# The order of one attention stage: value and gate projections together, the second front of the delta rule next, then the rotations and the attention

## The chip, the cores and the metric

One core of one Trainium2 chip runs the whole program in one launch. The metric is device time in microseconds (us), the median of the runs of a kernel. The engines named below are TensorE (PE, with its weight loads as PEld), VectorE (DVE), ScalarE (ACT), GpSimd (POOL) and SyncE (SP), whose queue issues nearly all DMAs.

## The reference

Two hybrid layers on 256 tokens of width 1024 come first, then one layer of a second kind, in which the change lies. Cut to what matters:

```python
zx = split(modulate(rmsnorm(x, g), ...) @ w_in)     # queries, keys, values, delta-rule inputs, gates
q, k = rmsnorm per head of zx[0], zx[1]; q, k = apply_axial_rope(q), apply_axial_rope(k)
o_a  = diff_attention(q, concat(k_ctx, k), concat(v_ctx, v), lam)     # 8 heads, two softmax maps each
scan_in = rwkv_prepare(zx[3], ...)                  # decay, kk, a, k, v, r of 16 heads, two directions
o_b  = rwkv_post(wkv_scan(s_ctx, scan_in), ...)     # s = s*w - (s@kk) (kk*a)^T + v k^T;  y = s @ r
x = x + mod * (sigmoid(g_a) * (o_a @ w_a) + sigmoid(g_b) * (o_b @ w_b)) @ w_out
x = x + mod * peer_ffn(...)                         # product-key experts, 128 x 128
```

## The kernel before

The program is written in the order of `body`: two layers of the first kind, then `second`, then the experts. The work of `second` on the main tokens runs in this order. `w_proj` and `z_proj` project the inputs of the delta rule and park them in DRAM (`zx`). The delta rule is done in two halves of eight heads, each by a `wkv_front` and a `wkv_back`:

- `wkv_front` (L1176) computes decays and keys for 8 blocks of 32 tokens in both directions, the Gram products of the blocks (L1300), the inverse of the 32 x 32 triangles by 31 elimination steps on DVE (a multiplication and a subtraction each, "the elimination" below; its input goes through DRAM as `din`, its result as `dout`, and L1333 transposes the result back), and the products that need the inverse.
- `wkv_back` (L1360) walks the 8 blocks in order, since the state `S` is carried. A step is L1376 (state times inputs, PE), an addition on DVE, L1392 (PE), an evacuation on ACT, L1404 (PE), and the addition and scaling of `S` on DVE. At the end L1420 adds what lies inside the blocks, and a group norm, L1446 and L1447 give the output `od`.

The attention has `da_front` (L1068: project and sum squares), `da_tail` (L1082: scale, rotate, transpose by L1108, store to DRAM), `v_unit` (L1126: 48 matmuls of 256 columns for a quarter of the values, stored to DRAM) and `gate2` (L1534: 48 matmuls, a tanh and one operation for an eighth of the gates). `diff_attention` (L1455) goes over 8 heads and two halves of the tokens, 16 items in all. An item's front is two score matmuls (L1476), two maxima (L1477), two exponentials (L1482), and L1488, which combines the two maps; its back is four transposes (L1494), an evacuation, four matmuls (L1499) and a scaling. The fronts run one item ahead of the backs. After the last item come a norm (L1520 to L1524), transposes (L1531) and the split into `hh` and `hl` (L394, L395), which `merge2` multiplies with `w_branch_a` ("ba"), then with `w_branch_b` ("bb").

In `second`, `da_tail` is a generator that yields after each quarter of the heads; the kernel before runs one `v_unit` after each quarter of the queries, and two `gate2` after each quarter of the keys. `wkv_front` and `wkv_back` are issued at a high priority, so the scheduler that sets the instruction order of each engine pulls them ahead as far as their buffers allow. Two buffers matter here: the second front writes its own `WR` into the tiles `hh` and `hl`, which the projections of values and gates read until their end, and it takes the tag `w8`, of which 9 buffers exist, so that a part of it waits until the first back has read its own.

Of the kernel before, what the change touches and what calls it, by code (L numbers as in the profile page):

```python
# [19 lines left out]
T = 256  # L20
# [174 lines left out]
class Kern:  # L195
# [1370 lines left out]
    def second(self, pool, xd):  # L1566
        nc, P = self.nc, self.P2
        self.rows2 = self.t(pool, [128, 384], "rows2")
        nc.sync.dma_start(self.rows2, self.A["rows2"].partition_broadcast(128))
        self.wkv_consts(pool)  # L1570
        dram = lambda shape, name: self.t(self.dram, shape, name)
        kTd, qTd, vd = dram([128, 8, 512], "kTd"), dram([128, 8, T], "qTd"), self.vd
        zx = dram([128, 24, T], "zx")
        gd, od = [dram([128, 8, T], f"gd{i}") for i in range(2)], dram([128, 8, T], "od")
        S = self.t(pool, [128, 2, 2, 4, 64], "S")
        for hf in range(2):
            nc.sync.dma_start(S[:, hf], self.Sd[hf])
        norm = lambda: [self.t(self.work, [128, 8, T], n, F32R) for n in ("hh", "hl")]
        hh, hl = self.ctx_front

        def back(state, S, od=None):
            with self.stream("r"), self.tc.high_priority(offset=30000):
                self.wkv_back(state, S, od)

        def front(*args):
            with self.stream("w"), self.tc.high_priority(offset=30000):
                return self.wkv_front(pool, *args)

        self.n4, self.n8 = 8, 9
        a = self.w8(pool, [128, 2, 16, 64])  # L1590
        fc = self.da_front(pool, a, "bk", hh, hl)
        nc.sync.dma_start(xd, self.x)
        hh, hl = norm()
        self.mod_norm(self.halves(self.x), P["norm1_g"], 0, 0, hh, hl, hold=True)
        wax, self.sg = self.w_proj(pool, 1, hh, hl)
        self.z_proj(pool, 1, hh, hl, zx)
        for _ in self.da_tail(pool, fc, self.rows2[:, 64:128], False, kTd, 0):
            pass
        st = front(1, 0, zx, wax)
        a = self.t(self.xp, [128, 2, 16, 64], "x")  # L1600
        fq = self.da_front(pool, a, "bq", hh, hl)
        a = self.t(self.xp, [128, 2, 16, 64], "xn", bufs=1)
        fk = self.da_front(pool, a, "bk", hh, hl)
        for i, _ in enumerate(self.da_tail(pool, fq, self.rope_tables(pool, self.rows2[:, 0:64], "tab"), True, qTd, 0)):
            self.v_unit(pool, i, hh, hl, vd, 2)
        for i, _ in enumerate(self.da_tail(pool, fk, self.rope_tables(pool, self.rows2[:, 64:128], "tab"), True, kTd, T)):
            for u in (2 * i, 2 * i + 1):
                g = self.gate2(pool, u, hh, hl)
                nc.sync.dma_start(gd[u // 4][:, 2 * (u % 4):2 * (u % 4) + 2], g)
        back(st, S[:, 0], od)  # L1610
        st = front(1, 1, zx, wax, True)
        hh, hl = norm()
        self.diff_attention(pool, kTd, qTd, vd, hh, hl)
        back(st, S[:, 1], od)
        M = self.t(self.xp, [128, 8, T], "xn", bufs=1)
        self.merge2(pool, M, "ba", gd[0], hh, hl)
        hh, hl = norm()
        for m in range(0, 8, 2):
            o = self.t(pool, [128, 2, T], "d2", bufs=4)
            nc.sync.dma_start(o, od[:, m:m + 2])  # L1620
            nc.scalar.activation(hh[:, m:m + 2], o, AF.Copy)  # L1621
            self.sub(hl[:, m:m + 2], o, hh[:, m:m + 2].bitcast(F32))
        self.merge2(pool, M, "bb", gd[1], hh, hl)
        hh, hl = norm()
        for m in range(0, 8, 2):
            nc.scalar.activation(hh[:, m:m + 2], M[:, m:m + 2], AF.Copy)
            self.sub(hl[:, m:m + 2], M[:, m:m + 2], hh[:, m:m + 2].bitcast(F32))
        self.x = self.t(self.xp, [128, 2, D], "x")
        nc.sync.dma_start(self.x, xd)
        g2 = [self.t(pool, [128, 512], "d2", bufs=4) for n in range(2)]  # L1630
        self.mod_rows(2, 0, g2)
        with self.stream("w"):
            pw = [self.bank_pair()]
        with self.stream("r"):
            pw.append(self.bank_pair())
        for i in range(4):
            self.linB_acc(f"bo{i}", pw, hh[:, 2 * i:2 * i + 2], hl[:, 2 * i:2 * i + 2], i == 0, i == 3)
        for t in range(2):
            for n in range(2):
                c = slice(512 * n, 512 * n + 512)  # L1640
                tp = self.t(pool, [128, 512], "d2", bufs=4)
                self.mul(tp, pw[t][n], g2[n])
                self.add(self.x[:, t, c], self.x[:, t, c], tp)
# [309 lines left out]
```

## Time and profile before

| what | value |
|---|---|
| median of 3 runs | 2797.48 us (2794.47 to 2798.41) |
| the profiled execution's own time | 2798.71 us |
| its span, first to last instruction | 2796.9 us |
| busy PE, PEld, DVE, ACT | 94%, 82%, 71%, 51% of the span |
| mean granted clock of TensorE | 0.946 of full speed |

The page says that PE is busy almost throughout, and that the mean clock is near full. A stage has to be read by itself: the page's row of granted clock shows two to four slices of forty well below full, and those lie in `second`, roughly from 1600 to 1800 us, where DMA moves less than half of what it moves elsewhere. The page's slices are 70 us wide, so finer windows are needed for the argument.

### The profile page before, as it was taken

Reading aid. Unit: us, or ns where it says so; the run is one execution under the profiler, and the core shown is the slowest. Engines: PE = TensorE matmul, PEld = TensorE weight load, DVE = VectorE, ACT = ScalarE, POOL = GpSimd, SP = SyncE. Lnnn points to the kernel's source line nnn. Section 1 sums busy time; section 2 is a strip of 40 time slices with the busy share of each in tenths; the row PEclk is TensorE's granted clock in tenths of the full one; section 3 lists DMA queues with packets and bytes.
Section 4 is the critical chain, followed back from the end, with each engine's and each line's share of the span. In section 5 each row is a group of like instructions: output and inputs, shape, how many; then the busy total and the mean of one; then the engine's idle time right before and its main releaser. Section 6 shows DMA issues by size and latency. Waiting matters only on the chain.

```text
span 2796.9 us, 54976 instructions
## 1 busy us (share of the span) xinstructions
PE 2635.9 (94%) x21856; PEld 2293.4 (82%) x21856; DVE 1978.4 (71%) x4085; ACT 1423.3 (51%) x2392; POOL 14.2 (1%) x45
## 2 busy tenths in 40 slices
PE   7999899999999999987998979989989999999999
PEld 7986588886997768877888755779989998888887
DVE  5996668765897658766788776566987765666665
ACT  4554446543555446534664655444446554444444
POOL 0000000000000000000000000000000000000000
PEclk9999999999999999988999976699999999999999
DMA  5532866546543555535746522264664346666665
GB/s 189 175 124 88 263 225 199 168 152 219 167 147 126 162 199 170 173 107 166 237 134 200 166 68 59 67 200 163 190 185 137 122 149 208 215 208 219 207 216 183
DMA packets 212433, 472.00 MB, mean 169 GB/s; under 512 B 52816, under 2 KB 86480, under 8 KB 211152
## 3 DMA queue, kind: packets, MB, share of 16 engines
q1 hardware_dynamic: 212176, 468.48, 52.4%
q8 instruction: 172, 2.82, 0.4%
q14 instruction: 85, 0.70, 0.1%
HBM read 427.77 MB, written 40.63 MB: 167 GB/s over the span
## 4 chain that ended last, share of the span: by engine, by line
PE 79%; DVE 10%; DMA 6%; ACT 4%; issue 2%; SPq 0%; DVEq 0%; ACTq 0%
PE a L333 8%; PE a L335 8%; PE a L334 8%; PE b L353 4%; PE b L351 4%; PE b L352 4%; PE b L1767 3%; PE x L335 3%; PE x L333 3%; PE x L334 3%; PE a L352 3%; PE a L351 3%; PE a L353 3%; DVE wl L277 3%; DMA raw<-in_peer 2%
## 5 line engine op out<-in xcount | busy, mean ns | idle before, releaser
L312 ACT ACTIVATE wh<-raw 128x1024 fp32r<-128x1024 f32 (+1 forms) x701 | 638.2, 913 | 689.3 <-PE a L334 247.4
L277 DVE TENSOR_TENSOR wl<-raw,wh 128x1024 fp32r<-128x1024 f32 (+1 forms) x701 | 727.4, 1041 | 357.9 <-ACT wh L312 332.6
L333 PE MATMUL a<-hh,wh 128*128 128x256 f32 x1920 | 550.2, 287 | 8.8 <-ACT hh L1621 4.1
L335 PE MATMUL a<-hh,wl 128*128 128x256 f32 x1920 | 549.5, 286 | 4.5 <-DVE wl L277 4.2
L334 PE MATMUL a<-hl,wh 128*128 128x256 f32 x1920 | 547.2, 285 | 0.6 <-DVE hl L277 0.5
L333 PEld LDWEIGHTS a<-hh,wh 128*128 128x128 f32 x1920 | 365.5, 190 | 22.0 <-ACT wh L312 4.9
L335 PEld LDWEIGHTS a<-hh,wl 128*128 128x128 f32 x1920 | 365.2, 190 | 14.8 <-DVE wl L277 9.0
L334 PEld LDWEIGHTS a<-hl,wh 128*128 128x128 f32 x1920 | 364.9, 190 | 5.4 <-DVE hl L277 0.7
L333 PE MATMUL x<-hh,wh 128*128 128x256 f32 x720 | 205.8, 286 | 5.6 <-ACT wh L312 5.2
L335 PE MATMUL x<-hh,wl 128*128 128x256 f32 x720 | 206.6, 287 | 3.0 <-DVE wl L277 3.0
L334 PE MATMUL x<-hl,wh 128*128 128x256 f32 x720 | 204.9, 285 | 0.0
L352 PE MATMUL b<-wl,ah 128*128 128x512 f32 x512 | 201.0, 393 | 0.0
L351 PE MATMUL b<-wh,ah 128*128 128x512 f32 x512 | 191.2, 393 | 2.8 <-issue 2.8
L353 PE MATMUL b<-wh,al 128*128 128x512 f32 x512 | 191.8, 391 | 0.0
L333 PEld LDWEIGHTS x<-hh,wh 128*128 128x128 f32 x720 | 137.2, 191 | 9.0 <-ACT wh L312 6.7
L335 PEld LDWEIGHTS x<-hh,wl 128*128 128x128 f32 x720 | 136.9, 190 | 5.7 <-DVE wl L277 4.4
L1802 ACT ACTIVATE ah<-pact 128x256 fp32r<-128x256 f32 x128 | 52.6, 412 | 173.1 <-PE b L352 160.3
L334 PEld LDWEIGHTS x<-hl,wh 128*128 128x128 f32 x720 | 137.1, 190 | 0.8
L352 PE MATMUL a<-wl,hh 128*128 128x256 f32 (+2 forms) x416 | 128.6, 309 | 8.0 <-DVE wl L277 7.9
L351 PE MATMUL a<-wh,hh 128*128 128x256 f32 (+2 forms) x416 | 125.3, 308 | 6.2 <-DVE hl L395 3.9
L277 DVE TENSOR_TENSOR wl<-rawv,wh 128x1024 fp32r<-128x1024 f32 x84 | 101.7, 1222 | 37.1 <-ACT wh L312 37.0
L353 PE MATMUL a<-wh,hl 128*128 128x256 f32 (+2 forms) x416 | 125.9, 304 | 0.0
(672 smaller groups left out, 5436.7 us busy)
## 6 DMA issues: line engine op xcount, KB each, us to landing
raw<-in_flat SPq DMA_DIRECT2D x289, 512.0 KB, 4.0
raw<-in_peer SPq DMA_DIRECT2D x172, 512.0 KB, 3.9
raw<-in_flat SPq DMA_DIRECT2D x228, 256.0 KB, 3.6
rawv<-in_peer SPq DMA_DIRECT2D x84, 512.0 KB, 4.6
TG<-in_flat SPq DMA_DIRECT2D x52, 512.0 KB, 5.9
parked<-act SPq DMA_DIRECT2D x89, 128.0 KB, 2.1
pact<-parked SPq DMA_DIRECT2D x89, 128.0 KB, 4.5
w<-vtd SPq DMA_DIRECT2D x32, 128.0 KB, 4.1
```

The source lines that it names most:

```text
L277: self.nc.vector.tensor_tensor(out, a, b, op=ALU.subtract)
L312: self.nc.scalar.activation(h, src, AF.Copy)
L333: mm(ps, wh[:, k], xh[:, k], start=first and k == 0, stop=False)
L334: mm(ps, wh[:, k], xl[:, k], start=False, stop=False)
L335: mm(ps, wl[:, k], xh[:, k], start=False, stop=last and k == nk - 1)
L351: mm(ps, xh[:, k], wh[:, k], start=first and k == 0, stop=False)
L352: mm(ps, xh[:, k], wl[:, k], start=False, stop=False)
L353: self.last = mm(ps, xl[:, k], wh[:, k], start=False, stop=last and k == nk - 1)
L1767: nc.tensor.matmul(ps[:, c], a[:, n, g, :, c], b[:, g, :, c], start=n == 0, stop=n == 2)
L1802: nc.scalar.activation(ah, act, AF.Copy)
```

## The change

The value projections are issued without the query rotations between them, and the gate projections without the key rotations. The rotations, both with their tables, are issued after the first back and the second front, just ahead of the attention.

```diff
--- before.py
+++ after.py
@@ -1601,14 +1601,17 @@
         fq = self.da_front(pool, a, "bq", hh, hl)
         a = self.t(self.xp, [128, 2, 16, 64], "xn", bufs=1)
         fk = self.da_front(pool, a, "bk", hh, hl)
-        for i, _ in enumerate(self.da_tail(pool, fq, self.rope_tables(pool, self.rows2[:, 0:64], "tab"), True, qTd, 0)):
+        for i in range(4):
             self.v_unit(pool, i, hh, hl, vd, 2)
-        for i, _ in enumerate(self.da_tail(pool, fk, self.rope_tables(pool, self.rows2[:, 64:128], "tab"), True, kTd, T)):
-            for u in (2 * i, 2 * i + 1):
-                g = self.gate2(pool, u, hh, hl)
-                nc.sync.dma_start(gd[u // 4][:, 2 * (u % 4):2 * (u % 4) + 2], g)
+        for u in range(8):
+            g = self.gate2(pool, u, hh, hl)
+            nc.sync.dma_start(gd[u // 4][:, 2 * (u % 4):2 * (u % 4) + 2], g)
         back(st, S[:, 0], od)
         st = front(1, 1, zx, wax, True)
+        for _ in self.da_tail(pool, fq, self.rope_tables(pool, self.rows2[:, 0:64], "tab"), True, qTd, 0):
+            pass
+        for _ in self.da_tail(pool, fk, self.rope_tables(pool, self.rows2[:, 64:128], "tab"), True, kTd, T):
+            pass
         hh, hl = norm()
         self.diff_attention(pool, kTd, qTd, vd, hh, hl)
         back(st, S[:, 1], od)
```

The scheduler decides the order on each engine, and it differs from about the first value unit to the merge of the second branch; before and behind that the two programs are in the same order. Three places show what moved.

DVE during the value projections, before. `w` is the elimination of the first front, `wl` a split of a weight piece, and `d`, `x` and `tab` are a rotation of a quarter of the queries:

```order
L271 TENSOR_TENSOR w_2455_15759<-w_2454_15756,w_2453_15754 128x252
L277 TENSOR_TENSOR wl_16720<-raw_16717,wh_16719 128x512
L271 TENSOR_TENSOR d_2597_16686<-x_16043,tab_16665 128x8x16 x4
L277 TENSOR_TENSOR w_2454_15756<-w_2454_15756,w_2455_15759 128x18x14
L1078 TENSOR_REDUCE dms_16355<-d_2593_16661 128x2x4
L277 TENSOR_TENSOR wl_16726<-raw_16723,wh_16725 128x512
L271 TENSOR_TENSOR x_16043<-x_16043,tab_16665 128x256 x2
L271 TENSOR_TENSOR w_2455_15759<-w_2454_15756,w_2453_15754 128x247
L1079 TENSOR_SCALAR dms_16355<-dms_16355 128x32
L274 TENSOR_TENSOR x_16043<-x_16043,d_2597_16686 128x256 x2
```

The rotation stands between the steps of the elimination and the splits. The same place in the change:

```order
L271 TENSOR_TENSOR w_2455_15759<-w_2454_15756,w_2453_15754 128x252
L277 TENSOR_TENSOR wl_16682<-raw_16679,wh_16681 128x512
L277 TENSOR_TENSOR w_2454_15756<-w_2454_15756,w_2455_15759 128x18x14
L1078 TENSOR_REDUCE dms_16355<-d_2593_16661 128x2x4
L277 TENSOR_TENSOR wl_16688<-raw_16685,wh_16687 128x512
L271 TENSOR_TENSOR w_2455_15759<-w_2454_15756,w_2453_15754 128x247
L1079 TENSOR_SCALAR dms_16355<-dms_16355 128x32
L277 TENSOR_TENSOR w_2454_15756<-w_2454_15756,w_2455_15759 128x19x13
```

All eight rotations (four of the queries, four of the keys) now come on DVE between the last gates and the eighth of the 31 steps of the second elimination. The scaling of queries and keys by their norms stays where it was.

PE in the last steps of the second back, before, around L1404 of the seventh step (`a_20179`):

```order
L1392 MATMUL a_20160<-w_2895_18904,w_2878_18650 32x64
L1392 MATMUL a_20160<-w_2896_18905,w_2878_18650 32x64
L1404 MATMUL a_20179<-w_2895_18904,w_2859_18555 64x64 x8
L1404 MATMUL a_20180<-w_2896_18905,w_2860_18556 64x64 x8
L1376 MATMUL a_20201<-S_13868,hh_18557 64x64
L1376 MATMUL a_20202<-S_13868,hh_18557 64x64
L1376 MATMUL a_20201<-S_13868,hl_18558 64x64
```

No attention is left there. The same place in the change:

```order
L1392 MATMUL a_20160<-w_2866_18715,w_2848_18460 32x64
L1499 MATMUL a_19582<-d_3058_19524,dt_19580 128x128 x4
L1476 MATMUL a_19596<-d_3080_19590,dq_19594 128x512
L1476 MATMUL x_19597<-d_3080_19590,dq_19594 128x512
L1404 MATMUL a_20179<-w_2865_18714,w_2829_18365 64x64 x8
L1404 MATMUL a_20180<-w_2866_18715,w_2830_18366 64x64 x8
L1494 MATMUL a_19612<-ident_61,x_19128 128x128 x4
L1376 MATMUL a_20201<-S_13868,hh_18367 64x64
L1376 MATMUL a_20202<-S_13868,hh_18367 64x64
```

Attention items now lie between the parts of every step of the second back, to its end. Counted on PE from the first L1392 of the second back to its last, 11 score matmuls (L1476) and the backs of 7 items lie there before, and 21 score matmuls and the backs of 11 items in the change.

PE behind the last L1392, before: L1420, the last transposes of the attention's result (L1531), then the merge (L333 to L335):

```order
L1392 MATMUL a_20227<-w_2896_18905,w_2878_18650 32x64
L1420 MATMUL a_20246<-w_2895_18904,w_2879_18651 32x64 x4
L1531 MATMUL x_19725<-ident_61,xn_19126 128x128 x4
L1420 MATMUL a_20313<-w_2895_18904,w_2879_18651 32x64 x3
L333 MATMUL a_20437<-hh_19116,wh_20433 128x256
L334 MATMUL a_20437<-hl_19117,wh_20433 128x256
L335 MATMUL a_20437<-hh_19116,wl_20434 128x256
```

In the change the last two items' backs and the output of the second half (L1446, L1447) come first:

```order
L1420 MATMUL a_20313<-w_2866_18715,w_2849_18461 32x64 x4
L1499 MATMUL x_19650<-d_3081_19592,dt_19648 128x128 x4
L1494 MATMUL a_19658<-ident_61,x_19128 128x128 x4
L1499 MATMUL a_19665<-d_3081_19592,dt_19663 128x128 x4
L1446 MATMUL a_20403<-ident_61,w_2883_18924 128x128 x2
L1447 MATMUL a_20404<-sgd_14283,w_2849_18461 128x256
```

The norm of the attention's result, its 16 transposes (L1531) and the merge follow behind them.

## Rows read from the trace of the kernel before

**Rows 1.** Seven windows: length; busy us of PE, PEld, DVE, ACT, POOL; clock; DMA; GB/s.

```profile
1486.40:1514.50 28.10, 21.71 (x162) 20.47 (x160) 26.45 (x85) 11.23 (x21) 0.00 (x0) 0.88 0.61 198
1514.50:1598.40 83.90, 81.68 (x936) 71.62 (x936) 60.90 (x137) 53.36 (x101) 0.00 (x0) 0.96 0.65 198
1598.40:1657.40 59.00, 53.46 (x980) 38.13 (x980) 42.06 (x99) 32.73 (x73) 1.11 (x2) 0.74 0.30 85
1657.40:1713.60 56.20, 40.74 (x314) 26.19 (x311) 49.07 (x125) 28.13 (x69) 0.00 (x0) 0.71 0.26 67
1713.60:1771.20 57.60, 55.10 (x523) 37.80 (x522) 28.93 (x74) 28.94 (x77) 0.00 (x0) 0.59 0.14 43
1771.20:1794.10 22.90, 18.49 (x273) 14.34 (x276) 11.72 (x34) 14.23 (x38) 0.00 (x0) 0.50 0.08 29
1794.10:1837.00 42.90, 37.33 (x487) 34.94 (x487) 27.58 (x50) 17.20 (x29) 1.89 (x1) 0.86 0.52 158
```

**Rows 2.** What PE waited for, 1440 to 1514.5 us: total, times, longest.

```profile
PE a L1108 <- DVE x L274: 4.9, 1, 4.9
```

**Rows 3.** Lines of DVE, 1440 to 1514.5 us: xcount, busy us, mean ns, idle before.

```profile
L271 DVE TENSOR_TENSOR d<-x,tab 128x128 f32<-128x128 f32 x16 | 3.6, 285 | 0.0
L274 DVE TENSOR_TENSOR x<-x,d 128x256 f32<-128x256 f32 x8 | 3.0, 424 | 0.0
L271 DVE TENSOR_TENSOR x<-x,tab 128x256 f32<-128x256 f32 x8 | 3.0, 420 | 0.0
```

**Rows 4.** Lines of PE, 1488 to 1493.6 us.

```profile
L352 PE MATMUL x<-wl,hh 128*128 128x256 f32 x16 | 4.5, 284 | 0.0
```

**Rows 5.** The timeline of DVE near 1597 and 1622 us: start, length, line, idle before.

```profile
1597.43 0.75 DVE L274 TENSOR_TENSOR S<-S,a 128x256 f32<-128x256 f32 x2
...
1622.26 1.23 DVE L1281 SCALAR_TENSOR_TENSOR w<-w,w 128x1024 f32<-128x1024 f32 x1 [0.91 <-PE a L1404]
```

**Rows 6.** Lines of DVE, 1598.4 to 1657.4 us.

```profile
L1488 DVE SCALAR_TENSOR_TENSOR x<-x,sm 128x512 f32<-128x512 f32 x4 | 3.0, 745 | 0.0
```

**Rows 7.** Lines of PE, 1713.6 to 1771.2 us.

```profile
L1476 PE MATMUL a<-d,dq 64*128 64x512 f32 x14 | 12.6, 996 | 0.0
L1499 PE MATMUL a<-d,dt 128*128 128x128 f32 x40 | 9.8, 421 | 0.0
L1404 PE MATMUL a<-w,w 64*64 64x64 f32 x160 | 8.4, 299 | 0.4 <-ACT w L268 0.4
L1392 PE MATMUL a<-w,w 32*32 32x64 f32 x129 | 8.1, 282 | 0.9 <-DVE w L274 0.8
L1476 PE MATMUL x<-d,dq 64*128 64x512 f32 x8 | 6.4, 891 | 0.8 <-ACT x L1482 0.8
L1376 PE MATMUL a<-S,hh 64*64 64x64 f32 x64 | 5.1, 319 | 0.0
L1494 PE MATMUL a<-ident,x 128*128 128x128 f32 x20 | 4.6, 370 | 0.5 <-DVE x L1488 0.5
L1376 PE MATMUL a<-S,hl 64*64 64x64 f32 x64 | 4.5, 318 | 0.0
L1499 PE MATMUL x<-d,dt 128*128 128x128 f32 x16 | 4.2, 441 | 0.0
L1494 PE MATMUL x<-ident,x 128*128 128x128 f32 x8 | 2.2, 431 | 0.0
```

**Rows 8.** The timeline of DVE, two updates of the state near the end.

```profile
1778.14 0.42 DVE L274 TENSOR_TENSOR S<-S,a 128x256 f32<-128x256 f32 x1 [2.13 <-PE a L1404]
...
1787.70 0.42 DVE L274 TENSOR_TENSOR S<-S,a 128x256 f32<-128x256 f32 x1 [3.60 <-PE a L1404]
```

**Rows 9.** The timeline of ACT at the attention's end, and of PE in the second merge.

```profile
1771.35 0.37 ACT L1501 ACTIVATE xn<-a,dr 128x128 f32<-128x128 f32 x1 [2.95 <-PE a L1499]
...
1777.56 4.78 ACT L1524 ACTIVATE xn<-xn,rs_y 128x128 f32<-128x128 f32 x16
...
1835.36 0.58 PE L333 MATMUL a<-hh,wh 128*128 128x256 f32 x1 [2.96 <-ACT hh L1621]
```

## The prediction

> **What bounds the kernel now.** I read the windows first, cut where the stages of the change begin and end: value units, gate units, the rest of the first back with the second front up to its elimination, the elimination, the second back in two parts, and the merge [rows 1]. The reader is to see two regimes. In the gate units PE is busy 81.68 of 83.90 us at a clock of 0.96: projections with the small matmuls of the delta rule between them, bound by PE. From 1598.4 on there are no projections. [...] The order of the delta rule's steps sets the end there, and the attention fills the gaps. In the value units it is DVE that is full, 26.45 of 28.10 us, while PE waits. The list of waits names the one that matters [rows 2]: 4.9 us in which the transposes of a rotated quarter wait for the rotation's last addition, with the next value unit behind them in PE's queue. The lines of PE and of DVE in single stretches then give the prices.
>
> **Part by part.** Eight rotations are moved. Four took 3.6 + 3.0 + 3.0 = 9.6 us of DVE [rows 3], so one is 2.4 us and all are 19.2. Each also brings four transposes on PE, an evacuation on ACT and a store on SP's queue.
>
> *Value units, -5.* A unit of 48 matmuls, 16 of each line, goes through in 5.6 us when nothing interrupts it: the window of [rows 4] holds exactly one. Four are 22.4 us, against 28.1 now [rows 1]. With 9.6 us of rotation gone, DVE has some 17 us of work there and no longer binds; one group of norm scalings stays, for which I give back 0.7. Bounds: -3, if that group still stops PE, and -9, if the 4.9 us come on top.
>
> *Gate units, -2.* PE binds, and DVE has 23 us to spare [rows 1], so the key rotations there were free. What goes is their 16 transposes on PE, some 0.12 us each at the pace of the projections (5.6 / 48). Bounds: 0 and -4. The stores of the rotated quarters, behind which weight loads queued on SP, go too; in a stage bound by PE that is worth nothing more.
>
> *First back and second front, +3.* The second front is not brought forward: its L1281 of the second direction waits for L1404 of the back's seventh step, before [rows 5] as in the change. Two steps of the back lie between the update at 1597.43 and 1622.26, 24.8 us; two undisturbed ones take 9.6 each [rows 8], so at most 5.7 are to be had when four items leave the stretch (DVE loses four L1488, 3.0 us [rows 6], and their maxima). But seven rotations, 16.8 us, come in, on a DVE that is busy 42.06 of 59.00, and the order puts a rotation ahead of the additions of both steps: 2 x 2.4, less about 2 for what no longer stands there. Bounds: -5, if the steps run undisturbed, and +9, if what comes in, less some 8 us that go, is paid in full.
>
> *Elimination, +1.* DVE is the bound (49.07 of 56.20 us to the start of the second back). One rotation comes in (2.4), one L1488 and a few small operations go (0.75 [rows 6] and some). Bounds: 0 and +6, if the first maxima, which stand between the steps, wait for keys that have just been stored and must be loaded again.
>
> *Second back, +17.* This is the main term. Before, the stretch of 57.6 us is PE's: its lines add up to 65.9 us, since records overlap, so each is scaled by 57.6 / 65.9 = 0.874 [rows 7]. The score matmuls, 19.0 us for 11 (each is recorded twice), come to 1.51 us each; the backs of 7 items, 14.0 + 6.8, to 2.60 each. The change has 21 and 11 between the same instructions (first to last L1392): 10 x 1.51 + 4 x 2.60 = 25.5 us more on PE. Against it stands the end of the stretch: 22.9 us in which the steps run alone, each waiting on itself [rows 1]. It holds three L1376, three L1392 and two L1404, 2.10, 1.77 and 1.47 us each by the same scaling, 14.5 us in all. The other 8.4 are gaps that items now fill. So 25.5 - 8.4 = +17. This takes the clock to stay at 0.59; bounds at other clocks are with the rivals, and +22 at 0.50.
>
> [...] The row shows PE busy 55.10 of 57.60 us at 0.59 [rows 1]. [...]
>
> *After the last step, +5.* The attention now ends behind the last L1392: two backs, 2 x 2.6, then the norm and the transposes, 11 us from the last scaling at 1771.35 to the end of L1524 at 1777.56 + 4.78 [rows 9], which before lay beside the last steps. That is +16. Against it, the output of the second half, which now holds up the second merge (PE waits 2.96 us for `hh` at 1835.36 [rows 9], and a clock of 0.86 over 42.9 us means about 12 us at half speed [rows 1]), gets done beside it: 3 for the wait, 3 for half of the 6 us the slow clock costs, 5 for the norm and the small matmuls. Bounds: 0 and +12.
>
> The sum is -5 - 2 + 3 + 1 + 17 + 5 = +19 us on 2798.7, the profiled execution's own time: 2817.7. That execution stands 1.2 above the median of the runs, so I predict 2816.5, rounded to 2816.
>
> **The rivals.**
> *The clock comes back.* If the fuller PE of the second back is granted more, its 97.5 us (80.5 + 17, 95.7% busy as in the row) shrink: at 0.70 to 93.3 x 0.59 / 0.70 + 4.2 = 83, a term of +2. Then the total is +4, 2801: no change. At 0.85 PE would need 69 us; eight steps at 9.6 are 77, less when their own PE part speeds up, so I take 70, a term of -10. The total is then -8, about 2789, on the other side. The point from which the sign turns is a mean clock of about 0.72 between the first and the last L1392 of the second back. For it: more and larger matmuls per us. Against it: 0.59 at 96% busy. [...]
> *The queues stand still.* DVE works in order, and the maxima of the first items stand between the steps of the elimination. If keys come late from DRAM, the elimination waits (+6 for +1), and if rotations delay the back in full, +9 for +3: together +11, 2827. For it: DVE has only 16.9 us free in the one stretch and 7.1 in the other [rows 1]. Against it: the rotation of the first keys lies well before the elimination in DVE's order.
> *All is cover.* If the attention only fills gaps in either place, the terms of the second back and of the end fall to what the front gains, and nothing moves: about 2797. The gaps are 8.4 us against 25.5 of work, so I put it with the case at 0.70.
>
> **How the numbers follow.** A measurement of this kernel can tell some 0.2%, 5.6 us, from no change. My forecast has 0.57, the standing queues 0.16, the half-returned clock or full cover 0.14, the full clock 0.13. That is 0.73 slower, 0.14 the same, 0.13 faster. The range takes in the forecast with its bounds, most of the queues' case and the upper part of the case of no change: 2798 to 2831. The forecast's own range is 2806 to 2828.
>
> **What would show it.** Value units of about 23 us with no wait of L1108 for DVE. Gates ending some 7 us earlier. The elimination starting 3 to 6 us earlier than now. From the first to the last L1392 of the second back about 97 us at a clock below 0.65, with L1476 to its end. The first matmul of the merge some 20 us behind the last L1392, and no wait for `hh` in the second merge. Wrong would be: that clock above 0.72; an elimination with waits for L1476; or a first stretch shortened by more than 10 us.

## The result, and the profile after

The changed kernel took 2810.43 us (median of 6 runs, 2805.53 to 2820.26); the kernel before, 2795.09 us in its runs on that occasion. The ratio is 1.0064, with a 95% interval of 1.0043 to 1.0085. A second set of 6 runs gave the same median and a ratio of 1.0062 (1.0045 to 1.0079). The sign was right, and 2810 us lies 6 us below the predicted 2816 and inside the range. What follows shows that the sum came out in part by luck, since terms on both sides were too small by about the same amount, and that a quantity which the prediction held fixed, the granted clock, differs between two executions of one kernel (0.60 and 0.68 in the second back of the change).

The windows of the profile after, cut at six events: the first matmul of the query projection, the first gate matmul, the last gate matmul, the first and the last L1392 of the second back, and the first matmul of L1058 behind both merges. Columns as in [rows 1].

```profile
1394.20:1498.30 104.10, 96.38 (x1161) 89.62 (x1162) 90.22 (x208) 64.78 (x114) 1.23 (x3) 0.97 0.50 151
1498.30:1574.70 76.40, 75.48 (x892) 66.16 (x892) 52.02 (x107) 48.63 (x95) 0.00 (x0) 1.00 0.62 197
1574.70:1690.20 115.50, 88.14 (x1228) 62.28 (x1228) 93.91 (x255) 53.19 (x107) 1.11 (x2) 0.63 0.28 84
1690.20:1792.30 102.10, 97.18 (x888) 61.49 (x891) 52.49 (x125) 48.34 (x130) 0.00 (x0) 0.60 0.14 37
1792.30:1868.60 76.30, 63.16 (x697) 59.85 (x696) 48.32 (x92) 36.76 (x74) 1.89 (x1) 0.93 0.55 181
```

The same five windows of a second profile of the kernel before (the run e11_before_again):

```profile
1401.80:1518.30 116.50, 102.08 (x1177) 94.76 (x1177) 99.89 (x247) 66.94 (x119) 1.23 (x3) 0.93 0.48 148
1518.30:1599.70 81.40, 80.57 (x906) 70.73 (x908) 58.64 (x133) 51.01 (x99) 0.00 (x0) 0.96 0.63 195
1599.70:1711.10 111.40, 87.45 (x1282) 60.22 (x1282) 88.66 (x221) 60.62 (x138) 1.11 (x2) 0.75 0.30 81
1711.10:1790.00 78.90, 68.78 (x837) 47.94 (x839) 45.36 (x116) 45.52 (x121) 0.00 (x0) 0.71 0.14 45
1790.00:1855.30 65.30, 59.55 (x662) 57.17 (x662) 41.41 (x71) 26.15 (x43) 1.89 (x1) 0.87 0.56 187
```

The reader is to see the first two windows get shorter and the last three longer. With both profiles of either kernel (all lengths are in the table below), the means change by -9.9 (to the first gate), -5.2 (gates), +6.3 (to the second back), +15.5 (second back) and +10.4 us (behind it): +17 in all. The first event itself comes at another time in each execution (1393.8 and 1398.3 us in two of one kernel, e4 and e7), which is why lengths of stages are compared here and not times from the span's start.

PE's waits of the changed kernel, 1440 to 1498.3 us. The wait of L1108 [rows 2] is gone; what is left, but for 0.6 us, is splits of weights:

```profile
PE a L352 <- DVE wl L277: 2.8, 3, 1.8
PE x L352 <- DVE wl L277: 1.6, 3, 0.9
```

The lines of PE, 1574.7 to 1690.2 us, show where that wait went. The 32 transposes of the rotated quarters now lie in the stretch of low clock (0.63), 9.8 us of busy time, and PE stands idle 8.7 us ahead of them for the rotations:

```profile
L1108 PE MATMUL a<-ident,xn 128*128 128x128 f32 x12 | 4.2, 452 | 5.9 <-DVE xn L274 5.9
L1108 PE MATMUL x<-ident,x 128*128 128x128 f32 x8 | 2.5, 436 | 2.4 <-DVE x L274 2.4
L1108 PE MATMUL a<-ident,x 128*128 128x128 f32 x8 | 2.4, 441 | 0.4 <-DVE x L274 0.4
L1108 PE MATMUL x<-ident,xn 128*128 128x128 f32 x4 | 0.7, 287 | 0.0
```

The same 32 in the kernel before, among the projections, 1440 to 1600 us, take 5.7 us:

```profile
L1108 PE MATMUL a<-ident,xn 128*128 128x128 f32 x16 | 2.8, 279 | 0.0
L1108 PE MATMUL a<-ident,x 128*128 128x128 f32 x8 | 1.5, 293 | 4.9 <-DVE x L274 4.9
L1108 PE MATMUL x<-ident,x 128*128 128x128 f32 x8 | 1.4, 271 | 0.0
```

The lines of PE in the second back, 1690.2 to 1792.3 us, which answer to [rows 7]: 44 records of score matmuls stand where 24 stand from first to last L1392 in the profile before, and the matmuls of the backs (L1499) take 64 + 24 records, where they take 64. Each of these matmuls is recorded twice, so these are 22 score matmuls and the L1499 of 11 items, against 12 and 8 before.

```profile
L1476 PE MATMUL a<-d,dq 64*128 64x512 f32 x28 | 26.7, 1051 | 1.2 <-ACT x L1482 1.2
L1392 PE MATMUL a<-w,w 32*32 32x64 f32 x256 | 15.7, 286 | 0.9 <-DMA w<-dout 0.7
L1499 PE MATMUL a<-d,dt 128*128 128x128 f32 x64 | 14.8, 403 | 0.0
L1476 PE MATMUL x<-d,dq 64*128 64x512 f32 x16 | 14.5, 1002 | 1.2 <-ACT dt L268 0.7 <-ACT x L1482 0.6
L1499 PE MATMUL x<-d,dt 128*128 128x128 f32 x24 | 6.2, 441 | 0.0
```

Behind the last step, ACT's timeline shows the norm of the attention's result, which in [rows 9] ends 12 us ahead of the last L1392, and PE's timeline what then waits:

```profile
1803.31 0.37 ACT L1501 ACTIVATE xn<-a,dr 128x128 f32<-128x128 f32 x1 [0.30 <-PE a L1499]
...
1807.94 4.79 ACT L1524 ACTIVATE xn<-xn,rs_y 128x128 f32<-128x128 f32 x16 [3.83 <-DVE rs_y L289]
```

```profile
1807.88 0.69 PE L1446 MATMUL a<-ident,w 128*128 128x128 f32 x2 [4.60 <-DVE w L271]
...
1816.47 0.66 PE L1531 MATMUL x<-ident,xn 128*128 128x128 f32 x4 [1.65 <-DVE hl L395]
1817.13 0.39 PE L333 MATMUL a<-hh,wh 128*128 128x256 f32 x1
...
1841.13 0.38 PE L333 MATMUL a<-hh,wh 128*128 128x256 f32 x1 [1.12 <-ACT hh L1624]
...
1845.86 0.38 PE L333 MATMUL a<-hh,wh 128*128 128x256 f32 x1 [1.59 <-ACT hh L1624]
```

The merge begins 24.9 us behind the last L1392 (1792.26), where it was 1.7 us (1794.11 to 1795.8), and the second merge still waits for `hh`, 2.7 us in two pieces.

### The profile page after: what moved, and what is told of

The parts are those of the page before. It is cut to its first block, busy times and chain, and to the rows that moved or that the text cites. A ratio compares the mean times of both kernels' runs of the same rounds, so it can differ in the third digit from the quotient of the medians.

```text
span 2806.0 us, 54967 instructions
## 1 busy us (share of the span) xinstructions
PE 2643.0 (94%) x21856; PEld 2294.3 (82%) x21856; DVE 1981.3 (71%) x4085; ACT 1424.9 (51%) x2392; POOL 14.3 (1%) x45
## 4 chain that ended last, share of the span: by engine, by line
PE 78%; DVE 10%; DMA 6%; ACT 4%; issue 2%; SPq 0%; DVEq 0%; ACTq 0%
PE a L333 8%; PE a L335 8%; PE a L334 8%; PE b L353 4%; PE b L351 4%; PE b L352 4%; PE b L1770 3%; PE x L335 3%; PE a L351 3%; PE a L352 3%; PE x L333 3%; PE x L334 3%; PE a L353 3%; DVE wl L277 2%; DMA raw<-in_peer 2%
## 5 line engine op out<-in xcount | busy, mean ns | idle before, releaser
L333 PE MATMUL a<-hh,wh 128*128 128x256 f32 x1952 | 558.9, 286 | 6.4 <-ACT wh L312 2.8
L335 PE MATMUL a<-hh,wl 128*128 128x256 f32 x1952 | 558.0, 286 | 4.0 <-DVE wl L277 3.7
L334 PE MATMUL a<-hl,wh 128*128 128x256 f32 x1952 | 556.0, 285 | 0.9 <-DVE hl L277 0.8
L333 PEld LDWEIGHTS a<-hh,wh 128*128 128x128 f32 x1952 | 371.8, 190 | 19.6 <-issue 4.3
L335 PEld LDWEIGHTS a<-hh,wl 128*128 128x128 f32 x1952 | 371.0, 190 | 12.4 <-DVE wl L277 6.4
L333 PE MATMUL x<-hh,wh 128*128 128x256 f32 x688 | 195.2, 284 | 6.3 <-ACT wh L312 6.1
L335 PE MATMUL x<-hh,wl 128*128 128x256 f32 x688 | 196.2, 285 | 4.1 <-DVE wl L277 4.1
L334 PE MATMUL x<-hl,wh 128*128 128x256 f32 x688 | 194.1, 282 | 0.0
L333 PEld LDWEIGHTS x<-hh,wh 128*128 128x128 f32 x688 | 129.8, 189 | 9.1 <-ACT wh L312 7.3
L335 PEld LDWEIGHTS x<-hh,wl 128*128 128x128 f32 x688 | 129.5, 188 | 8.0 <-DVE wl L277 7.0
L334 PEld LDWEIGHTS x<-hl,wh 128*128 128x128 f32 x688 | 129.4, 188 | 0.7
```

What stands on the lines that cost most here:

```text
L333: mm(ps, wh[:, k], xh[:, k], start=first and k == 0, stop=False)
L334: mm(ps, wh[:, k], xl[:, k], start=False, stop=False)
L335: mm(ps, wl[:, k], xh[:, k], start=False, stop=last and k == nk - 1)
```

## The experiments

Two tables hold the measurements. The first is of all timed runs. "Low" is the time at the lower of the two levels of the granted clock, the mean over the runs of 2 x span x (1 - mean clock). In windows of 2 us over the whole span, 1397 in each profile, the clock is 1.00 in 1222 and 0.50 in 122 before, 1.00 in 1230 and 0.50 in 127 in the change, and between the two only at a change of level. "Low" counts the whole kernel, and so also what lies outside the stages of the change.

| kernel | runs | median us | ratio to before (95%) | mean clock | low, us |
|---|---|---|---|---|---|
| before, beside the experiments | 78 | 2791.0 | | 0.952 | 267 |
| the change, both sets | 12 | 2810.4 | 1.0064, 1.0062 (above) | 0.947 | 298 |
| e1 rotations beside the gates | 10 | 2799.5 | 1.0035 (1.0017 to 1.0054) | 0.950 | 281 |
| e2 queries last | 6 | 2815.5 | 1.0090 (1.0074 to 1.0106) | 0.946 | 307 |
| e3 keys last | 6 | 2809.4 | 1.0057 (1.0037 to 1.0077) | 0.949 | 284 |
| e4, e7 attention held back | 13 | 2801.5 | e4: 1.0048 (1.0029 to 1.0067) | 0.949 | 286 |
| e6 the change and useless matmuls | 4 | 2808.1 | 1.0060 (1.0042 to 1.0077) | 0.955 | 253 |
| e8 no query rotation | 10 | 2793.6 | 1.0014 (0.9998 to 1.0030) | 0.950 | 282 |
| e9 before, useless matmuls in steps | 12 | 2787.7 | 0.9990 (0.9975 to 1.0005) | 0.955 | 250 |
| e10 before, useless matmuls in items | 12 | 2786.2 | 0.9982 (0.9967 to 0.9998) | 0.959 | 227 |
| e12 the change without rotations | 12 | 2799.3 | 1.0024 (1.0009 to 1.0040) | 0.948 | 292 |

The second is of the stages, from one profiled execution each, cut at the six events above: lengths in us, and for two of them the granted clock.

| kernel | to first gate | gates | to second back (clock) | second back (clock) | behind it |
|---|---|---|---|---|---|
| before, both profiles | 115.4, 116.5 | 81.6, 81.4 | 110.8 (0.74), 111.4 (0.75) | 87.2 (0.56), 78.9 (0.71) | 65.5, 65.3 |
| the change, both profiles | 104.1, 108.1 | 76.4, 76.3 | 115.5 (0.63), 119.2 (0.63) | 102.1 (0.60), 94.9 (0.68) | 76.3, 75.2 |
| e1 | 108.1 | 86.0 | 115.1 (0.69) | 83.1 (0.66) | 66.1 |
| e2 | 118.5 | 93.8 | 107.5 (0.71) | 101.4 (0.52) | 62.7 |
| e3 | 113.2 | 79.3 | 128.7 (0.68) | 90.9 (0.61) | 62.6 |
| e4, e7 | 116.2, 115.7 | 80.7, 81.1 | 106.6 (0.60), 106.8 (0.60) | 86.0 (0.81), 95.0 (0.68) | 77.4, 77.0 |
| e6 | 106.8 | 76.2 | 123.1 (0.67) | 90.0 (0.83) | 78.3 |
| e8 | 109.3 | 82.4 | 122.7 (0.72) | 82.7 (0.62) | 65.8 |
| e9 | 117.3 | 80.7 | 107.7 (0.81) | 92.4 (0.65) | 59.2 |
| e10 | 115.7 | 81.1 | 110.7 (0.71) | 78.3 (0.93) | 62.2 |
| e12 | 106.1 | 76.9 | 127.6 (0.69) | 95.3 (0.52) | 65.6 |

The first event is the first matmul of the query projection; the expectations call it, wrongly, the first projection of the delta rule's inputs.

**One part of the change at a time.** e1 takes the values bare and lays all eight rotations beside the gate units.

```diff
-        for i, _ in enumerate(self.da_tail(pool, fq, self.rope_tables(pool, self.rows2[:, 0:64], "tab"), True, qTd, 0)):
+        for i in range(4):
             self.v_unit(pool, i, hh, hl, vd, 2)
-        for i, _ in enumerate(self.da_tail(pool, fk, self.rope_tables(pool, self.rows2[:, 64:128], "tab"), True, kTd, T)):
-            for u in (2 * i, 2 * i + 1):
+        u = 0
+        for f in ((fq, 0, qTd, 0), (fk, 64, kTd, T)):
+            for _ in self.da_tail(pool, f[0], self.rope_tables(pool, self.rows2[:, f[1]:f[1] + 64], "tab"), True, f[2], f[3]):
                 g = self.gate2(pool, u, hh, hl)
...
+                u += 1
```

> Only the values run bare; the eight rotations lie beside the gate units, one quarter per unit, and back, second front and attention follow as before. On PE the second back then holds as many attention items as before (12 score matmuls and 8 backs between its first and last L1392). My theory is that the change is two separate effects: rotations beside the value units cost time because DVE is full there, and late attention costs time in the second back and behind it. It expects the first gate matmul 11 to 16 us earlier than before (near 1500), the gates at most 3 us longer than before, the second back from first to last L1392 near 82 us, and a total 8 to 14 us below before (about 2781 to 2787). The rival, that the rotations cost their DVE time wherever they stand, expects the gates longer by what the value units gain, and a total within 3 us of before.

The gates started 8 us earlier and then took 86.0 us, 4.5 more than before, where 3 at most was expected; the stretch behind them took 4 us more. The kernel was 8.5 us slower than before by the medians, which neither expectation had. The one profile does not show where, since it is of a faster execution (2792.6 us, against the median of 2799.5). The rival's reading is the nearer one: more than half of what the values gain is paid again in the gates.

e2 moves only the query rotations behind the second front, and its values are bare:

```diff
-        for i, _ in enumerate(self.da_tail(pool, fq, self.rope_tables(pool, self.rows2[:, 0:64], "tab"), True, qTd, 0)):
+        for i in range(4):
...
         st = front(1, 1, zx, wax, True)
+        for _ in self.da_tail(pool, fq, self.rope_tables(pool, self.rows2[:, 0:64], "tab"), True, qTd, 0):
+            pass
```

e3 moves only the key rotations, and its gates are bare:

```diff
-        for i, _ in enumerate(self.da_tail(pool, fk, self.rope_tables(pool, self.rows2[:, 64:128], "tab"), True, kTd, T)):
-            for u in (2 * i, 2 * i + 1):
+        for u in range(8):
...
         st = front(1, 1, zx, wax, True)
+        for _ in self.da_tail(pool, fk, self.rope_tables(pool, self.rows2[:, 64:128], "tab"), True, kTd, T):
+            pass
```

> The values run bare, the key rotations stay with the gates as before, and the query rotations come behind the second front, as in the change. Two more score matmuls and one more item's back than before lie between the first and last L1392 of the second back. My theory expects the gates to start 11 to 16 us earlier, the second back near 87 us instead of 82, the stretch behind its last L1392 at most 3 us longer, and a total 3 to 10 us below before. The rival, that rotations in the stretch of first back and second front cost time by taking DVE there, not by making the attention late, expects that stretch some 6 us longer and the second back unchanged.

> The values keep the query rotations, the gates run bare, and the key rotations come behind the second front, as in the change. Two more score matmuls and one more item's back than before lie in the second back. My theory expects the gates to start as before (within 3 us), the gates 2 to 4 us shorter, the second back near 87 us, and a total 0 to 6 us above before. The rival, that what the front gains comes from fewer rotations in all ahead of the gates' end, expects half of the change's 21 us here too, that is the end of the gates some 10 us earlier.

Both missed: each half of the change cost about as much as the whole (the medians are 24.5 and 18.4 us above before, that of the change 19.4). e3 kept its front as expected (113.2 and 79.3), and its second back was 91 us at 0.61, but the stretch ahead of it took 128.7 us. DVE's waits there, 1620.1 to 1715 us, point to the case called "the queues stand still": the maxima stand in DVE's queue between the steps of the elimination and wait for score matmuls that PE does late, 7.6 us in all.

```profile
DVE sm L1477 <- PE a L1476: 4.0, 2, 2.7
DVE sm L1477 <- PE x L1476: 3.6, 3, 2.0
```

Over the whole stretch from the last gate, these waits come to 11.4 us in e3, and to 3.1 and 4.3 us in the two profiles before. They are 7 to 8 of the 17 to 18 us by which the stretch is longer; what the rest is was not shown. The waits of e2 sum to 8.1 us, those of the change to 0.6: with all eight rotations moved, the first items come so late that hardly one stands in the elimination. e2 can't be split as cleanly, since steps of the first back move ahead of its gates' end (its first two windows hold 1226 and 1034 matmuls, those of the change 1161 and 892).

**Late attention alone.** e4, and e7 which is the same kernel once more, leave every rotation where it was and hold the first item back until the 13th step of the second elimination.

```diff
-            self.sub(X[:, 0:k + 1, k + 1:], X[:, 0:k + 1, k + 1:], p)
+            self.mark = nc.vector.tensor_tensor(X[:, 0:k + 1, k + 1:], X[:, 0:k + 1, k + 1:], p, op=ALU.subtract) if k <= 12 else self.mark
+            if k > 12:
+                self.sub(X[:, 0:k + 1, k + 1:], X[:, 0:k + 1, k + 1:], p)
...
-                cur = (h, t, *front(h, t))
+                with self.behind(None if prev else self.mark):
+                    cur = (h, t, *front(h, t))
```

> The order of before, rotations and all, but the first attention item is held back until the subtraction of the 13th elimination step of the second front, so that the attention starts as late as in the change (22 score matmuls and 11 backs between the first and last L1392 of the second back, two backs behind it). My theory, that late attention alone makes the second back long, expects the end of the gates as before, the stretch of first back and second front up to 3 us shorter, the second back near 97 us (82 before), the stretch behind it some 8 to 11 us longer, and a total 18 to 26 us above before. The rival, that the attention only fills gaps and the loss of the change comes from rotations beside the second front, expects a total within 4 us of before.

> The kernel with before's order and the attention held back, once more, for a second profile. If the clock of the second back differs from one execution to the next, this one has another clock than 0.81 there, and the stretch is as long as about 61 us of work at full speed make it: near 100 us at 0.60, near 86 at 0.81. If the clock belongs to this order of instructions, it is 0.81 within 0.04 again and 86 us within 3.

The second back and the last stretch, of e4:

```profile
1697.30:1783.30 86.00, 74.92 (x881) 48.81 (x881) 53.48 (x129) 48.69 (x132) 0.00 (x0) 0.81 0.18 53
1783.30:1860.70 77.40, 63.55 (x694) 59.70 (x694) 47.03 (x85) 35.87 (x71) 2.37 (x1) 0.89 0.52 175
```

and of e7:

```profile
1701.90:1796.90 95.00, 86.89 (x881) 56.05 (x881) 54.37 (x130) 49.25 (x132) 0.00 (x0) 0.68 0.16 48
1796.90:1873.90 77.00, 63.29 (x692) 59.17 (x693) 46.09 (x84) 35.28 (x69) 2.37 (x1) 0.89 0.52 176
```

Late attention alone costs about 10 us by the medians, half of what was expected and half of the change's loss. The price behind the last step is firm: 75 to 78 us in all five profiles with two backs behind it, 59 to 66 in all others. The price in the second back depends on the clock, and the clock differs between executions of one kernel. At nearly the same clock the term is about as forecast: 78.9 us at 0.71 before, 95.0 at 0.68 here and 94.9 at 0.68 in the change, 16 us more (12 against e1, which has as many items as before and takes 83.1 at 0.66). Busy PE times clock, the work at full speed, is 45 and 49 us before, 61 and 59 here, 58 and 60 in the change. In the 12 runs of e4 the time went from 2791.3 us at a mean clock of 0.957 to 2819.8 at 0.942.

> The changed kernel once more, for a second profile and more runs. Theory now, after the first four experiments: the length of the second back is the attention's matmuls in it (22 scores and 11 backs) times the granted clock, and the clock differs from one execution to the next (0.60 in the first profile of this kernel, 0.81 in the kernel with the attention held back, at the same counts, 102 and 86 us). It expects busy time of PE times clock in that stretch near 58 to 61 us again, whatever the clock, so 86 to 105 us, and the stretch behind it near 76 us. The rival, that the place of the rotations sets the second back, expects 102 us within 3 at whatever clock. Time: 2803 to 2813.

> The kernel before once more, for a second profile. Work of the second back (busy PE times granted clock) near 45 to 49 us, its length 80 to 92 us by the clock, the first gate matmul about 115 us behind the first projection of the delta rule's inputs, gates 81 us, and about 65 us from the last L1392 to the first matmul of L1058.

The second profiles of both kernels bore this out. The change: 94.9 us, 88.20 x 0.68 = 60 us of work. Before: 78.9 us, a little under the 80 expected, and 68.78 x 0.71 = 49. The place of the rotations does not set the second back.

```profile
1699.50:1794.40 94.90, 88.20 (x884) 55.87 (x887) 54.33 (x128) 48.45 (x130) 0.00 (x0) 0.68 0.15 42
```

**Work added on PE.** e6 adds one useless matmul to every item's back in the change, e10 the same in the kernel before; e9 adds smaller ones to the steps of the kernel before.

```diff
-            po = self.bank()[:, 0:128]
+            bk = self.bank()
+            po = bk[:, 0:128]
             for k in range(4):
                 mm(po, pT[:, k], ops[h][2][:, k], start=k == 0, stop=k == 3)
+            mm(bk[:, 128:512], pT[:, 3], ops[h][2][:, 0:3].rearrange("p k c -> p (k c)"), start=True, stop=True)
```

> The changed kernel with one useless matmul of 384 columns added to every attention item's back, written to columns of the bank that nothing reads. Ten of the sixteen lie between the first and last L1392 of the second back. At the pace of the score matmuls in the profile of before (1.51 us for 512 columns at 0.59) one is about 1.1 us. If PE's work binds the second back, it gets about 9 to 11 us longer and the kernel 8 to 16 us slower than the change. If the steps' own chain or DVE binds, it is within 3 us. If a fuller PE is granted the higher level, the second back has a clock above 0.75 and the kernel is no slower than the change, or faster.

> The kernel before, with the useless matmul of 384 columns in every attention item's back that the changed kernel had in the run before this. Ten of sixteen lie in the second back, six ahead of it. In the changed kernel it cost nothing (2808.1 against 2810.4) and the clock of the second back was 0.83. If that holds wherever attention fills the gaps, the second back here is within 4 us of before's, at a higher clock than 0.56 to 0.66, and the kernel within 5 us of before. If PE's work binds and the clock of that run was chance, it is 8 to 16 us slower.

> The kernel before, with useless 128x128 matmuls (two behind L1376, two ahead of L1404, two behind L1404) in steps 4 to 8 of the second back, written to columns of the step's own banks that nothing reads: 26 in all, about 0.25 us each at 0.59 by the transposes of the same shape, 6 us if all lay on the path. If the low clock in the end of the second back goes with PE standing still between the parts of a step, the granted clock there rises above 0.75 (0.50 in the last 23 us before), the stretch from first to last L1392 loses 4 to 12 us, and the kernel is 2 to 10 us faster than before. If the clock does not follow PE's own load, the stretch is 0 to 6 us longer and the kernel 0 to 6 us slower.

The second back and the added matmuls in it, of e6:

```profile
1698.00:1788.00 90.00, 82.60 (x892) 50.39 (x891) 50.50 (x125) 47.81 (x129) 0.00 (x0) 0.83 0.14 42
```

```profile
L1501 PE MATMUL a<-d,dt 128*128 128x384 f32 x15 | 7.9, 607 | 0.0
L1501 PE MATMUL x<-d,dt 128*128 128x384 f32 x6 | 4.5, 847 | 0.0
```

and the second back of e10:

```profile
1700.50:1778.80 78.30, 67.48 (x880) 43.29 (x880) 48.66 (x125) 46.82 (x128) 0.00 (x0) 0.93 0.20 60
```

PE got 12.4 us of records more in e6, and the second back was not longer: 90.0 us against 102.1 and 94.9. The clock was 0.83, hardly above the 0.81 of e4, and 0.93 in e10, above every profile without the addition. This is not one execution's luck: over its 12 runs e10 spent 227 us at the lower level against 267, and e6 over 4 runs 253 against the change's 298. e10 is also the one kernel here that is faster than the one before, 0.9982 (0.9967 to 0.9998), though by little. The scheduler ordered e10 anew, and its second back holds more attention than before: 16 score matmuls and the L1499 of 10 items, against 12 and 8. So the addition is not all that differs there. e9 is undecided: over its runs the time at the lower level fell to 250 us, but its one profile has the higher clock ahead of the second back (107.7 us at 0.81), where nothing was added, and not in it (92.4 us at 0.65), and its time can't be told from before.

A fuller PE did not go with a higher clock throughout. In the second back of the profile after, PE is busy 97.18 of 102.10 us at 0.60, so a full PE by the records is again not a fast one, as in the 55.10 of 57.60 us at 0.59 of [rows 1]; with the added matmuls it is busy 82.60 of 90.00 us at 0.83 in e6 and 67.48 of 78.30 us at 0.93 in e10.

**The rotations left out.** e8 leaves out the rotation arithmetic of the queries in the kernel before, e12 that of queries and keys in the change:

```diff
-            if rope:
+            if rope is True:
                 tmp = self.t(pool, [128, 2, 4, 64], "d2", bufs=4)
...
-        for _ in self.da_tail(pool, fq, self.rope_tables(pool, self.rows2[:, 0:64], "tab"), True, qTd, 0):
+        for _ in self.da_tail(pool, fq, self.rope_tables(pool, self.rows2[:, 0:64], "tab"), 2, qTd, 0):
```

> The kernel before, but the rotation of the queries is left out (neither sine nor cosine tables nor the gain are applied to them; scaling, transposes and stores stay where they are). It takes 9.6 us of DVE out of the value units and nothing off PE. If DVE is the bound there, the first gate matmul comes 7 to 11 us earlier than in before (counted from the first projection of the delta rule's inputs, 115.4 us in before). If only the one wait of L1108 was in the way, it comes 4 to 5 us earlier. If the matmuls and loads of the value units set the pace, under 3. The kernel's time: as much below before as the gates start earlier, if nothing gives it back; the kernel with the rotations beside the gates gave it back in the gates and behind them, so 0 to 8 us faster.

> The changed kernel without the arithmetic of the eight rotations (no sine, cosine or gain is applied to queries and keys; tables, scaling, transposes and stores stay). Without those 19 us on DVE the scheduler puts the attention as early as in before: 12 score matmuls and 8 backs in the second back, none behind it. So the front's gain of bare value and gate units stays and both costs, rotations beside the second front and late attention, are gone. Theory: the gates end 12 to 16 us earlier than in before (197 us behind the first projection of the delta rule's inputs), the stretch from there to the first L1392 is as in before (107 to 113 us), the second back 79 to 87, the last part 65, and the kernel 8 to 14 us faster than before. Rival: what the front gains is taken back before the second back in any case, as in the kernel with the rotations beside the gates and the one without the query rotation (115 and 123 us there); then the kernel is within 4 us of before.

e12 has the front of the change, no rotation on DVE, the attention as early as before, and is slower than before. The theory missed, and the rival was nearer, though it had 4 us at most and 8 were lost. Its stages from the gates' start:

```profile
1500.50:1577.40 76.90, 76.85 (x892) 67.88 (x892) 51.33 (x102) 48.94 (x95) 0.00 (x0) 0.98 0.63 195
1577.40:1705.00 127.60, 104.43 (x1309) 70.57 (x1308) 89.31 (x220) 65.47 (x147) 1.11 (x2) 0.69 0.29 86
1705.00:1800.30 95.30, 87.00 (x840) 59.09 (x844) 45.67 (x116) 46.10 (x121) 0.00 (x0) 0.52 0.16 42
```

The front's 15 us are there (106.1 and 76.9). The stretch behind holds the 32 transposes that came out of the projections and takes 127.6 us, and the second back, with as many items as before, takes 95.3 us at 0.52. Part of the longer stretch is again DVE's wait ahead of the maxima, from the last gate to the second back. Of e12:

```profile
DVE sm L1477 <- PE a L1476: 9.7, 5, 3.3
DVE sm L1477 <- PE x L1476: 1.7, 2, 0.9
```

and of before:

```profile
DVE sm L1477 <- PE x L1476: 3.1, 2, 1.6
```

The profiles with no rotation arithmetic in that stretch, and with the attention no later than before, line up by this wait: 107.7 us at none (e9), 110.8 at 3.1 and 111.4 at 4.3 (before), 115.1 at 4.4 (e1), 122.7 at 6.9 (e8), 127.6 at 11.4 (e12). Against before, the waits grew by 3 to 8 us in e8 and e12 and the stretch by 11 to 17, so they are a part of the loss and not all of it, and why the scores come later is open. In e8 the first gate came 6 to 7 us earlier, between what a full DVE was to give (7 to 11) and what the one wait would (4 to 5), so neither reading alone fits; the kernel gained nothing by it.

## Why the prediction was right, and where its steps were off

*Value units, -5.* The stretch to the first gate, which begins with the query projection, lost 9.9 us. The four value units alone, from their first matmul to the first gate, took 36.0 and 35.4 us before and 27.0 and 26.9 in the change: -8.7, at the edge of the bounds of -9 and -3. The direction held (no wait of L1108, and PE's idle time to the first gate fell from about 14 to 8 us), the term was mis-sized. The failing step is "Four are 22.4 us, against 28.1": the window of [rows 1] holds 162 matmul records, which three units of 48 fill with the transposes; four would need 192. One unit lay ahead of the window, with its rotation. By the prediction's own mark, a first stretch more than 10 us shorter would have made it wrong; the value units are just inside it.

*Gate units, -2.* Measured -5.2, just outside the bounds. Busy PE fell from 80.6 to 75.5 us and the clock rose from 0.96 to 1.00; at full speed that is 77.3 against 75.5, the -2 forecast, and the rest goes with the clock. e3, with bare gates alone, had 79.3.

*First back, second front and elimination, +3 and +1.* Measured +6.3 together, within the bounds. e4 and e7 split it: without early items the stretch is 106.7, 4.4 us less; the moved tails put 10.6 back. The working priced the rotations on DVE, but not the transposes in this stretch (9.8 us for 32, 0.31 us each) nor PE's 8.7 us of standing idle for them. It names the transposes as part of what each rotation brings, and prices them only among the projections, at 0.12 us each.

*Second back, +17.* Measured +15.5 as the mean of two profiles on either side, and +16 at nearly equal clock. The mechanism held, items times their price, less the gaps. The count was off by a part of a back: from first to last L1392 the trace has 12 score matmuls before and not 11, 22 in the change and not 21, the L1499 of 8 and 11 items, and the L1494 of 7 and 11. By the step's own prices that is 23.7 us more on PE and not 25.5, a term of +15. What the step took as given, a clock of 0.59, was no constant: 0.52 to 0.93 in fourteen profiles, and the 0.68 of the change's second profile lies above the prediction's mark of 0.65. Of the rivals, the clock did not come back: both profiles stay under the 0.72 at which the sign was to turn. The queues did not stand still: the elimination waited 0.6 us for score matmuls. And that all is cover is ruled out by e4 and e7, which pay for late attention alone.

*After the last step, +5.* Measured +10.4, within the bounds. The +16 was too small: the merge began 24.9 us behind the last L1392 and not 1.7, 23 us later. The two last backs ended 11.0 us behind it (1792.26 to 1803.28, with the L1420 between them), where 5.2 had been taken. What came off against it was about as forecast, some 13 us where 11 were expected, though not in every part: the second merge still waits 2.7 us for `hh` where 3 us were to go.

So a gain in front that was 8 us too small met two later costs that were 8 us too small, and the sum came out, +19 forecast and +17 in the profiles. The sign of every term was right and the second back's size too; that the misses of the others cancel is luck.

The clock ahead of the second back is the part that the working did not price. From before to the change, the mean span rose by 18.5 us (2789.3 to 2807.8), and the time at the lower level by 31 (267 to 298). What that is worth can be estimated from runs of one kernel: by a straight line through the runs of each kernel that has ten or more, the time grows by 0.25 to 0.44 us with each us at the lower level, which makes 8 to 14 us of the 18.5. It is not a second cause beside the terms: the transposes moved from projections at 0.93 (1486.4 to 1586.8 us of the profile before) into a stretch at 0.63 took 9.8 us there and not 5.7. But it is more than that, since e12 did less work, delayed no attention and still had 292. In the profiles most of the added low time lies between the last gate and the second back, 85 and 88 us in the change against 57 and 55 before (2 x length x (1 - clock)). What it costs there is open: e4 and e7 have 86 us too, and their stretch is the shortest of all.

Shown are the two gains in front, the price of late attention behind the last step and, at nearly equal clock, in the second back, and that the clock was higher over the runs with the matmul added to the items. Only inferred, as what is left, is the price of the moved rotations ahead of the second back. Not settled is why the time at the lower level grew whenever the front was shortened (281, 282, 284 and 292 us in e1, e8, e3 and e12): the kernels shorten it by different means, and none of the runs varies the clock by itself. With it stays open why e12, which has the gains and neither cost, is slower than before.

## What to carry to other kernels

Ask at which granted clock the place that work leaves and the place that it goes to run: the same 32 transposes took 9.8 us of PE's busy time in the stretch at 0.63, against 5.7 among the projections at 0.93. Time saved ahead of such a stretch need not be time saved at the end; here the front's 15 us were lost again even in a kernel that did less work and delayed nothing. Profile a kernel twice before reading a stage whose clock is not full.

## What the runs showed of the hardware that was not expected

In the second back, where PE's records are 87 to 95% busy before and in the change, a useless matmul in every attention item cost no time (2786.2 us in e10 against 2791.0 before, 2808.1 in e6 against 2810.4 in the change), and the granted clock was higher with it: 0.93 in e10 against 0.56 and 0.71 before, 0.83 in e6 against 0.60 and 0.68 in the change.

A fall of the clock is seen well in the changed kernel, behind the last step. In these windows (columns as above) PE stands still for 4.6 us, and then works without a gap at 0.50:

```profile
1803.30:1807.90 4.60, 0.02 (x1) 0.02 (x1) 4.53 (x24) 0.77 (x3) 0.00 (x0) 0.83 0.57 233
1807.90:1811.30 3.40, 3.40 (x12) 2.83 (x13) 0.01 (x1) 3.36 (x12) 0.00 (x0) 0.50 0.00 0
```

One kernel's second back, with the same instructions in the same order, took 86.0 us in one execution (e4) and 95.0 in another (e7), at 0.81 and 0.68.
